# Feed forward input products as seven half-size products instead of eight, two of the weight sums made by accumulating DMAs

## Chip, cores, metric

One core of one Trainium2 chip. The metric is the device time of one execution in microseconds (us); less is better. The program runs two blocks of a network one after the other; the change is in the second.

## What is computed

The second block works on 512 tokens of width 1024, two layers deep. Each layer has two gated feed forward stages (`ffn`), so four in all, and they are most of its work:

```
def swiglu(x, w_in, w_out):
    a, b = jnp.split(x @ w_in, 2, axis=-1)
    return (jax.nn.silu(a) * b) @ w_out
...
    for i in range(DEPTH_2):
        h = h + FFN_RES * swiglu(rmsnorm(h, g_ff1[i]), w_ff1_in[i], w_ff1_out[i])
        h = h + hybrid_mixer(rmsnorm(h, g_mix[i]), ...)
        h = h + FFN_RES * swiglu(rmsnorm(h, g_ff2[i]), w_ff2_in[i], w_ff2_out[i])
```

`w_in` is 1024 x 5632 (the first 2816 columns give `a`, the others `b`), `w_out` is 2816 x 1024.

## The kernel before

Everything lies transposed: features on the 128 partitions, the 512 tokens along the free dimension. A feature width is cut into tiles of 128, so the input product of a stage has 22 **blocks** `j` (2816 / 128), and a block has two projections, `a` and `b`, each of 8 tiles of the inner width 1024. The 22 blocks are two halves of 11. After each half comes the output product (`fo`): 8 output tiles of 11 matmul triples.

Every factor is a pair of a rounded part and a rest (`whi`/`wlo` of a weight, `xh`/`xl` of an activation), and a product is three matmuls, hi\*hi, hi\*lo, lo\*hi (`mm3`, lines 156 to 159). So a block is 2 x 8 x 3 = 48 matmuls with 512 moving columns.

Weights come from one packed array in the order of use. `Stream` loads a group of eight 128 x 128 tiles by one DMA (`wraw`, 512 KB) and makes two units of four tiles of it: ScalarE (ACT) casts the rounded part `whi` (line 108), VectorE (DVE) subtracts for the rest `wlo` (line 109). `wraw`, `whi` and `wlo` have three buffers each. `get` keeps one unit ahead of the matmuls. At the end of a block DVE scales both projections by the norm's factor `R`, ACT takes Silu, DVE multiplies, and the product is split again for the output product (lines 338 to 342, 169, 170).

A scheduler orders the instructions of each engine when the program is built; `high_priority` lets an instruction go ahead of others. On the chip each engine then runs its own list in that order, and waits at an instruction whose operands or buffers aren't ready.

Of the kernel before, what the change touches and what calls it, by code (L numbers as in the profile page):

```python
# [19 lines left out]
HALF = NFF // 2  # L20
GRP = 8
UNIT = 4
# [7 lines left out]
TAPS1 = (1, 1, 2, 1)  # L30
TAPS2 = 12
CONV_AT = 5
NEG = -float(2 ** 100)
EPS = 1e-6

# [47 lines left out]
class Stream:  # L83


    def __init__(self, tc, pool, dram, order, whole=()):
        self.tc, self.nc, self.pool, self.dram, self.order, self.whole = tc, tc.nc, pool, dram, order, whole
        self.i = 0
        self.units = {}
        self.raw = {}  # L90

    def _load(self, u):
        nc = self.nc
        if u * UNIT >= len(self.order) or u in self.units:
# [29 lines left out]

    def prefetch(self):
        self._load(self.i // UNIT)

    def group(self, g, dst):

# [48 lines left out]
def block2(tc, kk, W, h, xp, x0, sq0, p_t, par, out_t):  # L178


    nc = tc.nc
    with ExitStack() as ctx:
        cp = ctx.enter_context(tc.tile_pool(name="b2c", bufs=1))
        mp = ctx.enter_context(tc.tile_pool(name="b2m", bufs=1))
        gp = ctx.enter_context(tc.tile_pool(name="b2g", bufs=1))
# [20 lines left out]

        qk2 = [[[cp.tile([66, S], F32R, name=f"{n}2{b}{i}") for n in "qk"] for i in range(2)] for b in range(2)]
        ones2 = tmp("ones2")[64:66]  # L210
        nc.vector.memset(ones2, 1.0)
        for b in range(2):
            for i in range(2):
                nc.vector.tensor_copy(qk2[b][i][0][64:66], ones2)
        maskr = cp.tile([P, P], F32R, name="maskr")
        mt = tmp("mt", (P, P))
        nc.gpsimd.memset(mt, 0.0)
# [7 lines left out]
        st = K()  # L225
# [32 lines left out]
        def norm(sq=None, n=1024):  # L258
            sq = st.sq if sq is None else sq
            ps = paux("ssps")  # L260
            nc.tensor.matmul(ps, lhsT=kk.ones[n], rhs=sq, start=True, stop=True)
            R = cp.tile([P, S], F32, tag="R", name="R", bufs=2)
            rstd(R, ps)
            return R

        def proj(name, l, col, ps=None, k_n=KD, x=None):
            ps = psum("pj") if ps is None else ps
            x = (xh, xl) if x is None else x
            for k in range(k_n):
# [53 lines left out]

            return R, scale_h

        def ffn(l, wi, wo, after, first=False):
            if first:
                R, scale_h = first_norm()
            else:
                R = norm()  # L330
            for half in range(2):
                gh, gl = [], []
                for jj in range(HALF):
                    j = half * HALF + jj
                    pa = proj(wi, l, j * P)
                    pb = proj(wi, l, FF + j * P)
                    a = tmp("fa")
                    nc.vector.tensor_tensor(a, pa, R, op=ALU.mult)  # L338
                    nc.scalar.activation(a, a, AF.Silu)
                    b = tmp("fb")  # L340
                    nc.vector.tensor_tensor(b, pb, R, op=ALU.mult)  # L341
                    nc.vector.tensor_tensor(b, a, b, op=ALU.mult)
                    g1 = gp.tile([P, S], F32R, tag=f"gh{jj}", name=f"gh{jj}")
                    g2 = gp.tile([P, S], F32R, tag=f"gl{jj}", name=f"gl{jj}")
                    split(nc, g1, g2, b)
                    gh.append(g1)
                    gl.append(g2)
                    if first and j == 3:
                        scale_h()
                for m in range(KD):  # L350
                    ps = psum("fo")
                    for jj in range(HALF):
                        w = W.get((wo, l, (half * HALF + jj) * P, m * P))
                        mm3(nc, ps, w, (gh[jj], gl[jj]), jj == 0, jj == HALF - 1)
                    nc.vector.scalar_tensor_tensor(h[m], ps, 0.5, h[m], op0=ALU.mult, op1=ALU.add)
                    if half == 1:
                        after(m)

        def gt(i, hl, name):
            return gp.tile([P, S], F32R, tag=f"g{hl}{i}", name=name)  # L360

        def mixer(l, after):
            R = norm()
            oh = [gt(i, "h", f"oh{i}") for i in range(4)]
            ol = [gt(i, "l", f"ol{i}") for i in range(4)]
            ca = []
# [267 lines left out]
                    after(m)  # L634

        for l in range(2):
            ffn(l, "w_ff1_in_2", "w_ff1_out_2", lambda m: prep(m, "g_mix", l), first=l == 0)
            mixer(l, lambda m: prep(m, "g_ff2", l))
            ffn(l, "w_ff2_in_2", "w_ff2_out_2", lambda m: prep(m, "g_ple", l))
# [897 lines left out]
def tile_main(tc, xt, ctxt, w1, w2, p1, p2, rcnt, pt, out_t, off1, off2):  # L1537
    nc = tc.nc
    with ExitStack() as ctx:
        cp = ctx.enter_context(tc.tile_pool(name="cp", bufs=1))  # L1540
        wp = ctx.enter_context(tc.tile_pool(name="wp", bufs=1))
        hp = ctx.enter_context(tc.tile_pool(name="hp", bufs=1))
        xp = ctx.enter_context(tc.tile_pool(name="xp", bufs=1))
        kk = K()
        kk.sqp = cp
        kk.paroff = off2
        make_consts(tc, kk, cp)
        par = cp.tile([P, p2.shape[1]], F32, name="par2")
        nc.sync.dma_start(par, p2)
        W1 = Stream(tc, wp, w1, order1(), whole=("w_mod",))  # L1550
        W2 = Stream(tc, wp, w2, order2())
# [12 lines left out]
        block2(tc, kk, W2, h, xp, x0, sq0, pt, par, out_t)  # L1564

# [35 lines left out]
```

## Time and profile before

| | |
|---|---|
| median of 3 runs | 2983.14 us (2980.09 to 2984.42) |
| the profiled execution | 2981.43 us, of which its span 2979.7 us |
| granted TensorE clock, mean | 0.995 of 2.4 GHz |
| TensorE (PE) busy | 2934.9 us, 98% |
| DVE busy | 1910.1 us, 64% |
| ACT busy | 1298.3 us, 44% |

The span is from the first to the last instruction of the profiled execution. Busy is the union of an engine's instruction times; matmuls overlap in the pipeline of PE, so a single one lasts longer than the distance from one to the next.

### The profile page before, as it was taken

How to read it: one execution, taken by the hardware profiler on the slowest of the kernel's cores; microseconds unless marked ns; L12 is line 12 of the kernel's file. 1: busy time of each engine (PE TensorE's matmuls, PEld its weight loads, DVE VectorE, ACT ScalarE, POOL GpSimd, SP SyncE). 2: the span in 40 equal slices, each digit the busy share in tenths (PEclk: the TensorE clock that was granted, in tenths of full speed). 3: DMA queues.
4: the chain of work that ended last, by engine and by line, in shares of the span. 5: the costliest groups of instructions: out<-in, count | busy, mean ns of one | idle time of the engine just before them, and what ended most of it. 6: DMA issues, size and time to landing. Idle time of an engine off the chain costs nothing.

```text
span 2979.7 us, 37937 instructions
## 1 busy us (share of the span) xinstructions
PE 2934.9 (98%) x13992; PEld 2392.2 (80%) x13992; DVE 1910.1 (64%) x3753; ACT 1298.3 (44%) x2387; POOL 48.1 (2%) x105
## 2 busy tenths in 40 slices
PE   8999999999999999999999999999999999999998
PEld 5888887778888887688888888888888688888886
DVE  6788888787544469886543447444469886543446
ACT  6567766435323335544432335323335544432333
POOL 1000000000000000000000000000000000000000
PEclk9999999999999999999999999999999999999999
DMA  5211123233233332123333333333232123233332
GB/s 216 57 42 47 45 58 106 92 92 92 92 99 98 94 99 85 50 85 99 94 98 99 96 95 102 97 99 98 94 99 84 50 87 99 92 99 98 94 99 85
DMA packets 112986, 268.77 MB, mean 90 GB/s; under 512 B 43552, under 2 KB 47136, under 8 KB 112800
## 3 DMA queue, kind: packets, MB, share of 16 engines
q1 hardware_dynamic: 111776, 266.28, 28.8%
q8 instruction: 110, 1.80, 0.2%
q14 instruction: 76, 0.62, 0.1%
q0 software_dynamic: 1024, 0.07, 0.0%
HBM read 262.17 MB, written 4.06 MB: 89 GB/s over the span
## 4 chain that ended last, share of the span: by engine, by line
PE 93%; DVE 3%; ACT 2%; issue 1%; DMA 0%; SPq 0%; DVEq 0%; ACTq 0%
PE pj L158 17%; PE pj L157 17%; PE pj L159 17%; PE fo L158 5%; PE fo L157 5%; PE fo L159 5%; PE px L157 3%; PE px L158 3%; PE px L159 2%; PE o L486 1%; PE wo L158 1%; PE mX L1285 1%; PE wo L159 1%; PE mP L1290 1%; PE wo L157 1%; PE chn L1337 1%
## 5 line engine op out<-in xcount | busy, mean ns | idle before, releaser
L108 ACT CAST whi<-wraw 128x512 fp32r<-128x512 f32 x914 | 567.1, 621 | 1163.9 <-PE pj L158 699.3
L109 DVE TENSOR_TENSOR wlo<-wraw,whi 128x512 fp32r<-128x512 f32 x914 | 627.3, 687 | 446.1 <-ACT whi L108 423.6
L158 PE MATMUL pj<-xl,whi 128*128 128x512 f32 x1712 | 672.6, 393 | 0.0
L157 PE MATMUL pj<-xh,whi 128*128 128x512 f32 x1712 | 670.5, 392 | 0.9 <-DVE h L1526 0.9
L159 PE MATMUL pj<-xh,wlo 128*128 128x512 f32 x1712 | 669.3, 391 | 0.0
L159 PEld LDWEIGHTS pj<-xh,wlo 128*128 128x128 f32 x1712 | 321.9, 188 | 67.9 <-issue 2.3
L158 PEld LDWEIGHTS pj<-xl,whi 128*128 128x128 f32 x1712 | 322.2, 188 | 66.9 <-issue 2.7
L157 PEld LDWEIGHTS pj<-xh,whi 128*128 128x128 f32 x1712 | 322.2, 188 | 66.4 <-ACT whi L108 1.3
L157 PE MATMUL fo<-gh,whi 128*128 128x512 f32 x704 | 273.9, 389 | 0.0
L158 PE MATMUL fo<-gl,whi 128*128 128x512 f32 x704 | 273.9, 389 | 0.0
L159 PE MATMUL fo<-gh,wlo 128*128 128x512 f32 x704 | 273.9, 389 | 0.0
L420 DVE SCALAR_TENSOR_TENSOR cy<-ca,par,cy 128x489 f32<-128x489 f32 (+17 forms) x240 | 169.6, 729 | 1.5
L157 PE MATMUL px<-xh,whi 128*128 128x512 f32 x392 | 160.3, 409 | 0.8 <-ACT xh L1000 0.7
L158 PE MATMUL px<-xl,whi 128*128 128x512 f32 x392 | 160.6, 410 | 0.0
L159 PE MATMUL px<-xh,wlo 128*128 128x512 f32 x392 | 159.1, 406 | 0.0
L157 PEld LDWEIGHTS fo<-gh,whi 128*128 128x128 f32 x704 | 132.1, 188 | 27.5
L159 PEld LDWEIGHTS fo<-gh,wlo 128*128 128x128 f32 x704 | 132.1, 188 | 27.5
L158 PEld LDWEIGHTS fo<-gl,whi 128*128 128x128 f32 x704 | 132.1, 188 | 27.4
L341 DVE TENSOR_TENSOR fb<-pj,R 128x512 f32<-128x512 f32 x88 | 60.8, 691 | 129.9 <-PE pj L159 129.9
L338 DVE TENSOR_TENSOR fa<-pj,R 128x512 f32<-128x512 f32 x88 | 60.8, 691 | 125.4 <-PE pj L159 123.5
L157 PE MATMUL pj<-nh,whi 128*128 128x512 f32 x352 | 137.3, 390 | 0.0
L158 PE MATMUL pj<-nl,whi 128*128 128x512 f32 x352 | 137.0, 389 | 0.0
(427 smaller groups left out, 4473.4 us busy)
## 6 DMA issues: line engine op xcount, KB each, us to landing
wraw<-in_w_dram SPq DMA_DIRECT2D x465, 512.0 KB
mw<-in_w_dram SPq DMA_DIRECT2D x16, 512.0 KB
raw<-in_xt_dram SPq DMA_DIRECT2D x8, 256.0 KB
h<-in_xt_dram SPq DMA_DIRECT2D x8, 256.0 KB
out_dram<-fin SPq DMA_DIRECT2D x8, 256.0 KB
db<-B SPq DMA_DIRECT2D x64, 6.0 KB
Pm<-dq SPq DMA_DIRECT2D x64, 12.0 KB
Qm<-dq SPq DMA_DIRECT2D x64, 12.0 KB
```

The lines of the kernel that those rows point to most:

```text
L108: nc.scalar.copy(hi, src)
L109: nc.vector.tensor_tensor(lo, src, hi.bitcast(F32), op=ALU.subtract)
L157: nc.tensor.matmul(ps, lhsT=wh, rhs=xh, start=start, stop=False)
L158: nc.tensor.matmul(ps, lhsT=wh, rhs=xl, start=False, stop=False)
L159: nc.tensor.matmul(ps, lhsT=wl, rhs=xh, start=False, stop=stop)
L338: nc.vector.tensor_tensor(a, pa, R, op=ALU.mult)
L341: nc.vector.tensor_tensor(b, pb, R, op=ALU.mult)
L420: nc.vector.scalar_tensor_tensor(yy[:, s:], ca[cb][:, :S - s], pcol("conv_w", l, cb, j), yy[:, s:], op0=ALU.mult, op1=ALU.add)
L486: nc.tensor.matmul(po_[r, kb * P:], lhsT=vt[kb][:, hp * P + 64 * i:hp * P + 64 * i + 64], rhs=pts[i], start=kb == 0, stop=kb == 3)
L1285: nc.tensor.matmul(pX[:, o], lhsT=st.B[:, m0 + m], rhs=alt(st.Q, m0 + m), start=True, stop=True)
L1290: nc.tensor.matmul(pP[:, o], lhsT=Xt[:, m], rhs=alt(st.P, m0 + m), start=True, stop=True)
L1337: nc.tensor.matmul(pa, lhsT=st.kN[:, c], rhs=y2, start=True, stop=True)
```

## The change

Blocks 0 to 4 of each stage stay as they are (`plain`). From block 5 on, a block is one 2 x 2 product of matrices of halves: the weights' two projections (256 rows out) by the two halves of the inner width, times the activations' two halves of the inner width by the two halves of the tokens. It is computed by seven products of halves where eight were computed. A product is 4 inner tiles x 3 matmuls with 256 moving columns, so a block has 84 matmuls of 256.

- `operand(kk)`, four times per stage during the plain blocks, builds the activations' side: two normed tiles, four sums and differences of halves, and the splits of all (7 tiles each time).
- `squares` loads a block's weights: four plain loads on the SP queue (one of 512 KB, three of 256 KB), and two accumulating DMAs of 256 KB on the GpSimd (POOL) queue that add a quarter to the quarter already loaded (`s1`, `s3`). `weight` makes the other two sums on DVE (`s2`, `s4`) and splits each of the seven operands (128 x 512) on ACT and DVE. Their pairs go round eight buffers, which the plain blocks' activations held.
- `sevens` computes the seven products in the order a11, a12, s1, s2, s3, a22, s4, two to a PSUM bank (`sv`), and adds them up: ACT copies the first and the third out (`u`), DVE makes seven additions of 128 x 256, then ACT Silu, DVE multiply and split as before. Weights are prepared five products ahead in the text (`LEAD`).
- The second operands of the mixer (`qk2`) are set up anew in each mixer, since their buffers serve as operand buffers in between.

The number of columns streamed by PE falls from 48 x 512 to 84 x 256 per block, for 17 blocks in each of 4 stages: 68 blocks. Core of the diff:

```diff
+PLAIN = 5
+LEAD = 5
...
+    def squares(self, i, spare):
+        nc, g, H = self.nc, i // GRP, UNIT * P
+        x = self.pool.tile([P, GRP * P], F32, tag="wraw", name="wraw", bufs=3)
+        nc.sync.dma_start(x, self.dram[g])
+        s1 = self.pool.tile([P, H], F32, tag="whi", name="ws1", bufs=3)
+        nc.sync.dma_start(s1, self.dram[g + 1][:, :H])
+        s3 = spare()
+        nc.sync.dma_start(s3, self.dram[g][:, :H])
+        nc.gpsimd.dma_start(s1, self.dram[g + 1][:, H:], accum_op=ALU.add)
+        nc.gpsimd.dma_start(s3, self.dram[g + 1][:, :H], accum_op=ALU.add)
+        a22 = self.pool.tile([P, H], F32, tag="wlo", name="wa22", bufs=3)
+        nc.sync.dma_start(a22, self.dram[g + 1][:, H:])
+        return dict(a11=x[:, :H], a12=x[:, H:], s1=s1, s3=s3, a22=a22)
...
+            def operand(kk):
+                ab = []
+                for k in (kk, 4 + kk):
+                    t = tmp("xn")
+                    nc.vector.scalar_tensor_tensor(t, h[k], pcol(gname, l, k), R, op0=ALU.mult, op1=ALU.mult)
+                    ab.append(t)
...
+            def weight(j, name):
+                r = raws[j]
+                with tc.high_priority():
+                    if name == "s2":
+                        nc.vector.tensor_tensor(r["a11"], r["a11"], r["s1"], op=ALU.add)
+                        src = r["a11"]
+                    elif name == "s4":
+                        nc.vector.tensor_tensor(r["a12"], r["a12"], r["a11"], op=ALU.add)
+                        src = r["a12"]
+                    else:
+                        src = r[name]
+                    hi, lo = pair(turn[0] % 8, alt)
+                    turn[0] += 1
+                    split(nc, hi, lo, src)
+                return hi, lo
+
+            def sevens(js, half, at, then):
+                steps = [(n, name) for n in range(len(js)) for name in ("a11", "a12", "s1", "s2", "s3", "a22", "s4")]
...
+                for i in range(LEAD):
+                    prepare(i)
+                for i, (n, name) in enumerate(steps):
+                    prepare(i + LEAD)
...
+                    if name in ("a11", "s1", "s3", "s4"):
+                        bank[:] = [psum("sv") if turns[0] % 2 else paux("sv"), 0]
+                        turns[0] += 1
+                    o = bank[0][:, H * bank[1]:H * bank[1] + H]
...
+                    for kk in range(4):
+                        w = slice(kk * P, kk * P + P)
+                        mm3(nc, o, (wh[:, w], wl[:, w]), ops[rhs[name], kk], kk == 0, kk == 3)
+                    if name == "a11":
...
+                        nc.scalar.copy(u1, o)
+                    elif name == "a12":
+                        nc.vector.tensor_tensor(h1, o, u1, op=ALU.add)
+                    elif name == "s1":
+                        nc.scalar.copy(u2, o)
+                    elif name == "s2":
+                        nc.vector.tensor_tensor(u1, o, u1, op=ALU.add)
+                        nc.vector.tensor_tensor(h2, u1, u2, op=ALU.add)
+                    elif name == "s3":
+                        nc.vector.tensor_tensor(v1, o, u1, op=ALU.add)
+                        nc.vector.tensor_tensor(v2, v1, u2, op=ALU.add)
+                    elif name == "a22":
+                        nc.vector.tensor_tensor(v1, o, v1, op=ALU.add)
+                    else:
+                        nc.vector.tensor_tensor(h2, o, h2, op=ALU.add)
+                        nc.scalar.activation(st.h, st.h, AF.Silu)
+                        nc.vector.scalar_tensor_tensor(st.h, st.v, -1.0, st.h, op0=ALU.mult, op1=ALU.mult)
+                        hidden(js[n] - half * HALF, st.h)
...
             for half in range(2):
...
+                for j in range(lo_, min(PLAIN, lo_ + HALF)):
+                    if j == PLAIN - 1:
+                        load(js[0], first_at)
+                    plain(j - lo_, j)
+                    if j < 4:
+                        operand(j)
                     if first and j == 3:
                         scale_h()
+                sevens(js, half, first_at, out_at)
```

**How the lists of the engines change.** First PE, inside the second half of the first stage. Before, a block was 48 matmuls in a row with one wait per unit. Now PE's list mixes the products: the end of a11 of one block (`xh6` is its weight pair's rounded part), eight matmuls of s1 (`xh0`), then the first of a12 (`xh7`), into the bank `sv_10186` that a11 filled.

```order
L185 MATMUL sv_10186<-xs_8181,xl6_10086 128x256
L183 MATMUL sv_10235<-sl1_7871,xh0_10121 128x256
L184 MATMUL sv_10235<-sh2_7880,xh0_10121 128x256
L185 MATMUL sv_10235<-sl1_7871,xl0_10122 128x256
L183 MATMUL sv_10235<-sh5_7984,xh0_10121 128x256
L184 MATMUL sv_10235<-sl5_7985,xh0_10121 128x256
L185 MATMUL sv_10235<-sh5_7984,xl0_10122 128x256
L183 MATMUL sv_10235<-xs_8089,xh0_10121 128x256
L184 MATMUL sv_10235<-xs_8090,xh0_10121 128x256
L183 MATMUL sv_10186<-sl0_7867,xh7_10103 128x256 [waits Activation_49]
```

The last row waits for ACT, though its weights were cast before those of s1: it waits for the copy out of its bank.

ACT, before, around a block of the feed forward: casts of the stream's units, one Silu, one split.

```order
L339 ACTIVATE fa_13805<-fa_13805 128x512 [waits DVE_49]
L108 CAST whi_13816<-wraw_13787 128x512 [waits PE_49,Activation_49]
L108 CAST whi_13834<-wraw_13832 128x512 [waits DMAHW0_49,PE_49,Activation_49]
L169 CAST gh5_13811<-fb_13808 128x512 [waits DVE_49]
L108 CAST whi_13851<-wraw_13832 128x512 [waits PE_49,Activation_49]
```

And now, at the place of the PE rows above. `xh4`, `xh6`, `xh7`, `xh0` are casts of the weights of s4 of this block and a12, s1, s2 of the next; `u_10199` are the two copies out of PSUM.

```order
L195 CAST xh4_10204<-wraw_9929 128x512 [waits PE_49]
L195 CAST xh6_10249<-wraw_10075 128x512 [waits PE_49,Activation_49]
L501 COPY u_10199<-sv_10186 128x256 [waits PE_49]
L195 CAST gh3_10178<-hid_10054 128x512 [waits DVE_49]
L195 CAST xh7_10267<-ws1_10077 128x512 [waits DMASW5_49,PE_49,Activation_49]
L195 CAST xh0_10287<-wraw_10075 128x512 [waits PE_49,Activation_49]
L505 COPY u_10199<-sv_10235 128x256 [waits PE_49]
```

Each copy stands behind a cast into the pair that a product just ending on PE still reads (pairs go round by eight, so the cast of a12 of the next block takes the pair of a11 of this one).

DVE at the same place: between the addition that reads s2 (line 507) and the one that reads s3 (line 510) stand the sum behind it and two splits for the next block.

```order
L507 TENSOR_TENSOR u_10199<-sv_10235,u_10199 128x256 [waits DVE_49,PE_49,Activation_49]
L508 TENSOR_TENSOR hid_10200<-u_10199 128x256 [waits DVE_49]
L196 TENSOR_TENSOR xl1_10305<-s3_10079,xh1_10304 128x512 [waits DMASW0_49,Activation_49]
L196 TENSOR_TENSOR xl2_10329<-wa22_10083,xh2_10328 128x512 [waits DMAHW6_49,PE_49,Activation_49]
L510 TENSOR_TENSOR v_10201<-sv_10271,u_10199 128x256
```

Last, DVE at the passage from block 4 (plain) to block 5 in the very first stage: `xl6_8528` and `xl7_8546` are weights of block 7, `fa_8291` and `fb_8294` read the results of plain block 4, `hid_8350` is the first addition of block 5, `xl1_8418` the rest of s1 of block 6.

```order
L196 TENSOR_TENSOR xl7_8546<-wraw_8371,xh7_8545 128x512 [waits PE_49,Activation_49]
L351 TENSOR_TENSOR h3_5812<-h3_5812,Rh_8202 128x512
L454 TENSOR_TENSOR wraw_8371<-wraw_8371 128x512 [waits DVE_49]
L351 TENSOR_TENSOR h4_5814<-h4_5814,Rh_8202 128x512
L351 TENSOR_TENSOR h5_5816<-h5_5816,Rh_8202 128x512
L351 TENSOR_TENSOR h6_5818<-h6_5818,Rh_8202 128x512
L351 TENSOR_TENSOR h7_5820<-h7_5820,Rh_8202 128x512
L431 TENSOR_TENSOR fa_8291<-pj_8227,R_7769 128x512
L434 TENSOR_TENSOR fb_8294<-pj_8262,R_7769 128x512
L435 TENSOR_TENSOR fb_8294<-fa_8291,fb_8294 128x512 [waits DVE_49,Activation_49]
L196 TENSOR_TENSOR gl4_8298<-fb_8294,gh4_8297 128x512 [waits Activation_49]
L503 TENSOR_TENSOR hid_8350<-sv_8336,u_8349 128x256 [waits PE_49]
```

The scaling of `h`, which before lay inside a long row of plain blocks, now stands between weights of a block far ahead and the first results that PE's banks wait to be read.

## Rows read from the trace of the kernel before

**Rows 1.** The page's first part: engine, busy us, share of the span, instructions.
```profile
PE 2934.9 (98%) x13992; PEld 2392.2 (80%) x13992; DVE 1910.1 (64%) x3753; ACT 1298.3 (44%) x2387; POOL 48.1 (2%) x105
```

**Rows 2.** The page's 40 equal slices: busy tenths of PE, granted clock.
```profile
PE   8999999999999999999999999999999999999998
...
PEclk9999999999999999999999999999999999999999
```

**Rows 3.** The chain that ended last, as shares of the span.
```profile
PE 93%; DVE 3%; ACT 2%; issue 1%; DMA 0%; SPq 0%; DVEq 0%; ACTq 0%
```

**Rows 4.** Timeline within one feed forward block: start us, us long, engine, line, operation.
```profile
1502.36 0.39 PE L158 MATMUL pj<-xl,whi 128*128 128x512 f32 x1
...
1502.84 0.62 ACT L108 CAST whi<-wraw 128x512 fp32r<-128x512 f32 x1 [1.19 <-PE pj L158]
...
1503.49 0.69 DVE L109 TENSOR_TENSOR wlo<-wraw,whi 128x512 fp32r<-128x512 f32 x1 [1.91 <-ACT whi L108]
...
1506.34 0.68 DVE L109 TENSOR_TENSOR wlo<-wraw,whi 128x512 fp32r<-128x512 f32 x1
...
1506.94 0.68 DVE L342 TENSOR_TENSOR fb<-fa,fb 128x512 f32<-128x512 f32 x1
...
1507.66 0.62 ACT L169 CAST gh<-fb 128x512 fp32r<-128x512 f32 x1 [1.49 <-DVE fb L342]
...
1508.28 0.62 ACT L108 CAST whi<-wraw 128x512 fp32r<-128x512 f32 x1
...
1508.31 0.69 DVE L170 TENSOR_TENSOR gl<-fb,gh 128x512 fp32r<-128x512 f32 x1 [0.69 <-ACT gh L169]
...
1510.74 0.39 PE L159 MATMUL pj<-xh,wlo 128*128 128x512 f32 x1
...
1510.97 0.39 PE L157 MATMUL pj<-xh,whi 128*128 128x512 f32 x1
...
1511.17 0.69 DVE L338 TENSOR_TENSOR fa<-pj,R 128x512 f32<-128x512 f32 x1 [1.54 <-PE pj L159]
```

**Rows 5.** Timeline of PE in the first block, matmuls of 256 columns.
```profile
60.74 0.28 PE L157 MATMUL pc<-cx,whi 128*128 128x256 f32 x1
60.85 0.28 PE L158 MATMUL pc<-cx,whi 128*128 128x256 f32 x1
60.97 0.28 PE L159 MATMUL pc<-cx,wlo 128*128 128x256 f32 x1
61.09 0.40 PE L157 MATMUL px<-xh,whi 128*128 128x512 f32 x1
```

**Rows 6.** Groups by form, operations of 256 columns: count, busy us, mean ns.
```profile
L831 ACT COPY u<-pc 128x256 f32<-128x256 f32 x16 | 5.8, 371 | 6.3 <-PE pc L159 3.7 <-PE chn L1324 2.5
L1229 DVE TENSOR_TENSOR B<-B,KK 128x256 f32<-128x256 f32 x8 | 3.3, 410 | 0.0
```

**Rows 7.** Timeline of DVE, two operations of which the second reads the first.
```profile
1098.01 0.69 DVE L255 SCALAR_TENSOR_TENSOR rs<-ssps,rs 128x512 f32<-128x512 f32 x1
1098.74 0.69 DVE L256 SCALAR_TENSOR_TENSOR R<-rs,R 128x512 f32<-128x512 f32 x1
```

**Rows 8.** Timeline, a matmul whose weights DVE makes at the last moment.
```profile
502.50 0.34 DVE L1330 SCALAR_TENSOR_TENSOR rhs<-chn,negeG,vN 128x128 f32<-128x128 f32 x1
...
502.90 0.30 PEld L1333 LDWEIGHTS chn<-rhs,Pm 128*128 128x128 f32 x2 [0.36 <-DVE rhs L1330]
502.90 0.49 PE L1333 MATMUL chn<-rhs,Pm 128*128 128x128 f32 x2
503.11 0.30 PEld L1350 LDWEIGHTS po<-y,QK 128*128 128x128 f32 x2
```

**Rows 9.** Busy time in one feed forward stretch: PE, PEld, DVE, ACT, POOL, clock, DMA share, GB/s.
```profile
725.00:840.00 115.00, 114.75 (x521) 95.27 (x522) 62.22 (x112) 42.68 (x68) 0.50 (x2) 1.00 0.29 92
```

**Rows 10.** DMA issues on POOL's queue: size, median us to landing.
```profile
k<-cs POOLq DMA_DIRECT2D x32, 2.0 KB, 1.6
```

More of the change, by code (lines that the diff above doesn't have):

```diff
@@ L324, in first_norm, with pair, extra, ffn @@
             return R, scale_h
-        def ffn(l, wi, wo, after, first=False):
+        def pair(i, alt):
+            if alt:
+                return mtile(2 * i, f"sh{i}"), mtile(2 * i + 1, f"sl{i}")
+            return tuple(xp.tile([P, S], F32R, tag=f"x{n}{i}", name=f"x{n}{i}") for n in "hl")
+        def extra(i):
+            tags = [f"{n}2{b}{j}" for b in range(2) for j in range(2) for n in "qk"] + ["pe3", "pe3", "cs", "x28"]
+            return cp.tile([P, S], F32R, tag=tags[i], name="xs", bufs=2 if tags[i] == "pe3" else 1)
+        def ffn(l, gname, wi, wo, after, first=False, alt=False):
             if first:
@@ L330, in ffn @@
                 R = norm()
-            for half in range(2):
[L332 to L347, printed above, removed]
+            H = S // 2
@@ new lines, in ffn, with slot @@
+            ops = {}
+            base = W.i
+            used = []
+            def slot():
+                n = len(used)
+                used.append(n)
+                if n < 16:
+                    if n % 2 == 0:
+                        used_pair[:] = pair(n // 2, not alt)
+                    return used_pair[n % 2]
+                return extra(n - 16)
+            used_pair = []
+            def operand(kk):
[4 more added lines that the diff above has]
+                    ab.append(t)
+                x, y = ab
+                b11, b12, b21, b22 = x[:, :H], x[:, H:], y[:, :H], y[:, H:]
+                t = slot()
+                split(nc, t[:, :H], t[:, H:], b11)
+                ops["b11", kk] = t[:, :H], t[:, H:]
+                hi, lo = slot(), slot()
+                split(nc, hi, lo, y)
+                ops["b21", kk] = hi[:, :H], lo[:, :H]
+                ops["b22", kk] = hi[:, H:], lo[:, H:]
+                u = tmp("t12")
+                nc.vector.tensor_tensor(u[:, :H], b11, b12, op=ALU.subtract)
+                nc.vector.scalar_tensor_tensor(u[:, H:], u[:, :H], -1.0, b22, op0=ALU.mult, op1=ALU.subtract)
+                v = tmp("t34")
+                nc.vector.tensor_tensor(v[:, :H], b22, b12, op=ALU.subtract)
+                nc.vector.scalar_tensor_tensor(v[:, H:], u[:, H:], -1.0, b21, op0=ALU.mult, op1=ALU.subtract)
+                for t, names in ((u, ("t1", "t2")), (v, ("t3", "t4"))):
+                    hi, lo = slot(), slot()
+                    split(nc, hi, lo, t)
+                    ops[names[0], kk] = hi[:, :H], lo[:, :H]
+                    ops[names[1], kk] = hi[:, H:], lo[:, H:]
@@ new lines, in hidden, with plain @@
+            def hidden(jj, g):
+                g1 = gp.tile([P, S], F32R, tag=f"gh{jj}", name=f"gh{jj}")
+                g2 = gp.tile([P, S], F32R, tag=f"gl{jj}", name=f"gl{jj}")
+                split(nc, g1, g2, g)
+                gs[jj] = g1, g2
+            def plain(jj, j):
+                pa = proj(wi, l, j * P)
+                pb = proj(wi, l, FF + j * P)
+                a = tmp("fa")
+                nc.vector.tensor_tensor(a, pa, R, op=ALU.mult)
+                nc.scalar.activation(a, a, AF.Silu)
+                b = tmp("fb")
+                nc.vector.tensor_tensor(b, pb, R, op=ALU.mult)
+                nc.vector.tensor_tensor(b, a, b, op=ALU.mult)
+                hidden(jj, b)
@@ new lines, in ffn, with load @@
+            raws = {}
+            def load(j, at):
+                if j not in raws:
+                    raws[j] = W.squares(at, lambda: cp.tile([P, S], F32, tag="R", name="s3", bufs=2))
+            turn = [0]
+            def weight(j, name):
[13 more added lines that the diff above has]
+                return hi, lo
@@ new lines, in sevens, with prepare @@
+            def sevens(js, half, at, then):
+                steps = [(n, name) for n in range(len(js)) for name in ("a11", "a12", "s1", "s2", "s3", "a22", "s4")]
+                rhs = dict(a11="b11", a12="b21", s1="t1", s2="t2", s3="t3", s4="b22", a22="t4")
+                ready = {}
+                live = {}
+                bank = []
+                turns = [0]
+                def prepare(i):
+                    if i < len(steps):
+                        n, name = steps[i]
+                        if name == "a11":
+                            for q in (n, n + 1):
+                                if q < len(js):
+                                    load(js[q], at + 16 * q)
+                        ready[i] = weight(js[n], name)
+                for i in range(LEAD):
+                    prepare(i)
+                for i, (n, name) in enumerate(steps):
+                    prepare(i + LEAD)
+                    if i == len(steps) - 7:
+                        W.ahead(then)
+                    st = live.setdefault(n, K())
+                    if name in ("a11", "s1", "s3", "s4"):
+                        bank[:] = [psum("sv") if turns[0] % 2 else paux("sv"), 0]
+                        turns[0] += 1
+                    o = bank[0][:, H * bank[1]:H * bank[1] + H]
+                    bank[1] += 1
+                    wh, wl = ready.pop(i)
+                    for kk in range(4):
+                        w = slice(kk * P, kk * P + P)
+                        mm3(nc, o, (wh[:, w], wl[:, w]), ops[rhs[name], kk], kk == 0, kk == 3)
+                    if name == "a11":
+                        st.u, st.h, st.v = tmp("u"), tmp("hid"), tmp("v")
+                        u1, u2, h1, h2, v1, v2 = (t[:, e * H:e * H + H] for t in (st.u, st.h, st.v) for e in range(2))
+                        nc.scalar.copy(u1, o)
[16 more added lines that the diff above has]
+                        hidden(js[n] - half * HALF, st.h)
+                        live.pop(n)
+                W.i = then
@@ new lines, in ffn @@
+            for half in range(2):
+                gs = {}
+                lo_ = half * HALF
+                js = list(range(max(lo_, PLAIN), lo_ + HALF))
+                out_at = base + (half + 1) * HALF * 16 + half * KD * HALF
+                first_at = out_at - 16 * len(js)
+                for j in range(lo_, min(PLAIN, lo_ + HALF)):
[4 more added lines that the diff above has]
+                        operand(j)
@@ L348, in ffn @@
                     if first and j == 3:
                         scale_h()
+                sevens(js, half, first_at, out_at)
                 for m in range(KD):
+                    if half == 0 and m == KD - 1:
+                        load(HALF, out_at + KD * HALF)
                     ps = psum("fo")
@@ L363, in mixer @@
             R = norm()
+            qk2 = second_operands()
             oh = [gt(i, "h", f"oh{i}") for i in range(4)]
```

31 lines of the change are left out of this document (19 added, 12 removed).

## The prediction

> **What bounds the kernel now.** The page's first part comes first: PE is busy 98% of the span, DVE 64%, ACT 44% [rows 1]. The slices show PE at 9 tenths everywhere at a full clock [rows 2], and the chain of work that ended last lies on PE for 93% [rows 3]. So nothing but PE's own work counts, and the question is how densely PE issues matmuls. The timeline within a block answers it: from the L158 at 1502.36 to the L157 at 1510.97 are 38 matmuls of 512 columns, 0.2267 us each [rows 4]. A block of 48 takes 10.88 us, and no engine makes PE wait in it: ACT's cast at 1502.84 was released by a matmul, not the other way round. In that stretch DVE is busy 54% and ACT 37% of the time [rows 9]: both have room, which the change is about to use.
>
> **The change, part by part.**
>
> *Matmuls.* 84 of 256 columns replace 48 of 512. Three in a row in the first block take 61.09 - 60.74 = 0.35 us, 0.1167 each [rows 5]; half of 0.2267 would be 0.1134. I take 0.1167, a measured distance of that very form: 84 x 0.1167 = 9.80 us per block, 1.08 less than 10.88, times 68 blocks **-73.4 us**. With 0.1134 it is -92, with 0.120 -54. At 0.1295 nothing would be won. [...]
>
> *DVE and ACT.* Queued DVE operations of 512 columns start 0.60 apart (1506.34, 1506.94) though each lasts 0.68 [rows 4]; one of 256 lasts 0.41 [rows 6], so 0.33 apart; one that reads the operation just before starts 0.73 after it [rows 7], 0.04 after its end. Per new block DVE has 7 splits, 2 sums, a multiply and a last split (11 x 0.60) and 7 additions (7 x 0.33 and 0.12 for the one that waits): about 9.0 us. ACT has 9 casts and splits or Silu at 0.62 and 2 copies at 0.37 [rows 4, 6]: 6.3 us. Neither is above PE's 9.80, but both must now answer PE several times in each block.
>
> *New waits.* The lists show three kinds per block: a12 waits for ACT's copy of a11, s2 for the copy of s1, a22 for DVE's reading of s3. None is for data that the product uses; two products share a bank. I price each as the path from PE's last release to the waiting matmul, less the matmuls that stand between in PE's list. The pieces: a matmul of 256 lasts 0.28 [rows 5]; ACT starts 0.09 after the end of the matmul that frees its buffer (1502.36 + 0.39 to 1502.84), DVE 0.04 after (1510.74 + 0.39 to 1511.17) [rows 4]; PE resumes 0.06 after DVE (502.50 + 0.34 to 502.90) [rows 8].
> - a12: the cast of the next a12 can start when a11's eleventh matmul ends, and the copy stands behind it: 0.28 + 0.09 + 0.62 + 0.37 + 0.06 = 1.42 us. From that matmul's start PE has 2 + 8 matmuls to do: 1.17. Wait 0.25.
> - s2: from a12's eleventh: two casts, then the copy, 0.37 + 1.24 + 0.37 + 0.06 = 2.04, against 2 + 4 + 9 matmuls, 1.75. Wait 0.29.
> - a22: from s2's last: 0.32 to DVE, line 507 and its dependent 508 (0.45 + 0.33), two splits (1.20), line 510 (0.41), 0.06: 2.77, against 1 + 3 + 12 + 7 matmuls, 2.68. Wait 0.09.
>
> Sum 0.63. The order repeats every three blocks; in the other two ACT's Silu and further casts stand ahead of the copies. At a12 the path grows by two and by three of them, to 2.67 and 3.29, and PE has 19 and 24 matmuls to cover it (2.22 and 2.80). At s2 it is 1.61 from a12's start against 12 (1.40), and 2.04 against 14 (1.63). At a22 2.87 against 24 and 2.77 against 23. They wait 0.45 + 0.21 + 0.07 and 0.49 + 0.41 + 0.09. Mean 0.78 per block: **+53 us** over 68. DVE keeps up in this timetable, with about 1.5 us idle per block.
>
> *Restart.* Where a wait holds the weight load too, the first matmul comes one load later: the pair of loads in [rows 8] lasts 0.30, one 0.19, so 0.11 per wait. In an unheld stream the load runs ahead. The waiting matmuls here have old weights, so I take 0; the other bound is 3 x 0.11 x 68 = +22.
>
> *Passage from the plain blocks.* In the first stage ACT's first copy (u of block 5) stands behind casts for blocks 6 and 7. By the same pieces PE stops 1.2 us at a12 of block 5. Then s2 needs the second copy, which follows the Silu of plain block 4, which follows `fa`, which follows line 351 five times and a sum, which follow `xl7`; and that split ends about when a12 does. Six operations of 0.60, `fa`, Silu and copy with 0.7, 0.65 and 0.4 make some 5.1 us of waiting; with 1.2 in front and behind, 7.5. The other stages have no line 351 there: 0.75 us for the last operand splits and 1.95 at a12, behind four casts and a Silu, 2.7 each. Together **+15.6**; no row of before shows this, so between 8 (half) and 24 (half more).
>
> *Ends of the halves.* The last block has no next one to fill its waits: some 0.3, eight times, **+2.4**.
>
> *Operands.* 4.9 us of DVE per plain block for four blocks, on top of 4.8 (8 operations at 0.60): 9.7 of 10.88. Hidden, since the stream's splits stay a unit ahead in DVE's list; if that cover goes, at most 4 us per stage.
>
> *Transfers.* A plain block loads 0.5 + 0.5 MB, a new one 1.3 MB by plain loads and 0.5 MB by accumulating ones. At the stretch's price, 0.29 of the DMA engines for 92 GB/s [rows 9], 1.83 MB in 10.6 us take 0.54 of them. The s3 buffers (two) are freed some 20 us before they are needed, and I see POOL's small DMAs land in 1.6 us [rows 10]. No row shows an accumulating one; at the price of a load it costs nothing, at four times it 0.29 x (1.31 + 4 x 0.52)/(92 x 10.6/1000) = 1.0, and the engines are full: there it begins to decide. The Trainium skill (DMA: Bandwidth & Descriptors, section Anatomy of one DMA) fits 2.0 us + bytes / 436 GB/s for a DMA from GpSimd; by this estimate a load and an accumulation take 5.2 us, well within the buffers' time. No run here has shown it.
>
> *Sum:* -73.4 + 53 + 15.6 + 2.4 = **-2.4 us**, 2979.0 against the profiled execution's 2981.43, which is 1.7 below the median shown; say **2980**.
>
> **Rivals.** *A, the forecast:* the waits give back nearly all. Its own range takes 0.1134 and 0.120 per matmul (faster matmuls wait longer: about half of the difference stays, -9 and +9) and the passages: 2964 to 2996.
> *B, the waits are covered:* if ACT's and DVE's releases come earlier than my pieces (0.25 us at each wait would do for the first kind), only passages and ends remain: -73.4 + 18 = -55, **2926**; half covered 2953. For it: the scheduler put 8 to 14 matmuls in just these gaps. Against it: every piece is measured.
> *C, slower by the restart:* each of the nine waits in three blocks costs a weight load as well, 0.11 us. It decides above 0.04 us per wait; in full it gives -2.4 + 22 = +20, **3001**. For it [rows 8]; against it, that there the late operand is the weight.
> *D, the accumulating DMAs are the bound:* at 4.6 times a load's price they fill 11.7 us per block, 1.1 over the 10.6 of A, +75: **3055**. Against it the 20 us between.
> *E, the products aren't cheaper:* 0.1295 or more per matmul of 256. [Rows 5] speak against it; it is within D's chance.
>
> **How the numbers follow.** A 0.45 (of that 0.15 faster, 0.20 same, 0.10 slower), B 0.27, C 0.18, D with E 0.10. Faster by over 0.2% (6 us, about what a measurement tells from no change): 0.15 + 0.27 = 0.42. Same 0.20. Slower 0.10 + 0.18 + 0.10 = 0.38. The range must leave out no more than 0.2: D is left out above (0.10) and the fully covered end of B below (about 0.08): 2930 to 3015.
>
> **What would show it.** Per block: the distance of `sv` matmuls where nothing waits (0.1134 to 0.120); the time of three blocks in the second half (31.7 us by A, 29.4 by B, 32.7 by C); idle PE before L183 released by ACT `u` and DVE `v`; the restart in the load after such a wait. In the first stage a gap of about 5 us on PE some 3 us after it starts a12 of block 5, released by ACT `u`. DMA share near 0.54 in the second halves, and no DVE wait on L451 released by a DMA. The prediction is wrong if PE's matmuls of 256 columns last longer beside so much DVE and DMA work, if DVE falls behind by more than its 1.5 us, or if the banks aren't what a12 waits for.

## The result, and the profile after

The changed kernel takes **3036.78 us** (median of 4 runs, 3033.17 to 3038.93), the kernel before 2981.98 in the same session: ratio 1.0182, 95% interval 1.0164 to 1.0200. The forecast was 2980 with a range of 2930 to 3015, so it missed, and on the slow side. The profiled execution took 3033.17 us, its span is 3031.5 against 2979.7: 51.8 us more.

The page of the changed kernel, busy times, slices of PE and clock, and one row on DMA issues:

```profile
PE 2923.4 (96%) x16440; PEld 2488.6 (82%) x16440; DVE 2269.3 (75%) x4598; ACT 1468.2 (48%) x2791; POOL 166.0 (5%) x241
...
PE   8999999999899999999999999999999999999998
...
PEclk9999999999999999999999999999999999999999
...
ws<-in_w_dram POOLq DMA_DIRECT2D x68, 256.0 KB, 5.3
```

PE is busy 11.5 us less than in [rows 1], and yet the span grew. The slices, which answer to [rows 2], hide why: what PE lost is in gaps too short for a slice of 76 us. So the stretches of sevens have to be measured one by one, each from its first `sv` matmul to the first `fo` matmul behind it. First the four first halves (6 blocks each), then the four second halves (11 blocks), by windows; columns as in [rows 9]:

```profile
780.35:858.96 78.61, 67.13 (x505) 65.11 (x504) 61.44 (x116) 33.94 (x64) 10.39 (x12) 0.91 0.55 145
...
sum 292.36, PE 258.84 PEld 253.35 DVE 230.86 ACT 136.35 POOL 41.49; mean PE 64.71 PEld 63.34 DVE 57.72 ACT 34.09 POOL 10.37
```
```profile
1633.78:1759.42 125.64, 117.66 (x926) 114.19 (x924) 100.09 (x193) 61.01 (x116) 15.59 (x18) 0.97 0.58 146
...
sum 500.00, PE 471.23 PEld 457.13 DVE 401.13 ACT 244.52 POOL 62.31; mean PE 117.81 PEld 114.28 DVE 100.28 ACT 61.13 POOL 15.58
```

292.36 + 500.00 = 792.4 us for 68 blocks; at 10.88 each they took 739.8 before. That is +52.5, the whole difference: it lies in these eight stretches and nowhere else. The mean clock in them is 0.91 to 0.97, not 1.00.

Inside a second half, away from its start, PE's timeline shows a wait as this pattern:

```profile
1672.98 0.28 PE L184 MATMUL sv<-sh,xh 128*128 128x256 f32 x1
...
1676.69 0.19 PEld L184 LDWEIGHTS sv<-xs,xh 128*128 128x128 f32 x1
1676.81 0.28 PE L184 MATMUL sv<-xs,xh 128*128 128x256 f32 x1
1676.99 0.19 PEld L183 LDWEIGHTS sv<-sl,xh 128*128 128x128 f32 x1
1676.99 0.38 PE L183 MATMUL sv<-sl,xh 128*128 128x256 f32 x1
1677.21 0.28 PE L184 MATMUL sv<-sh,xh 128*128 128x256 f32 x1
1677.33 0.28 PE L185 MATMUL sv<-sl,xl 128*128 128x256 f32 x1
...
1700.51 0.28 PE L184 MATMUL sv<-sh,xh 128*128 128x256 f32 x1
```

From 1672.98 to 1676.81 are 32 matmuls without a wait: 0.1197 us each. The matmul at 1676.99 comes 0.18 after the one ahead (0.06 of waiting), the next 0.22 after that (0.10 more). The weight load of the waiting matmul is held with it: it starts at 1676.99 too, where the load before it starts 0.12 ahead of its matmul. Three blocks, from 1668.79 to 1700.51 at the same place of the pattern, take **31.72 us**. In them are nine such pairs: the waits sum to 0.65 us, the longer distances behind them to 0.91. The window over the three:

```profile
1668.79:1700.51 31.72, 31.72 (x254) 30.69 (x253) 27.97 (x55) 17.48 (x34) 5.22 (x6) 1.00 0.72 174
```

At the start of each half it looks different. The timeline of a second half, all engines, some matmuls of PE left out (PE began the sevens at 1633.78):

```profile
1628.70 0.86 POOL L148 DMA_DIRECT2D ws<-in_w_dram  x1 [53.12 <-PE fo L185]
...
1631.03 0.33 SPq L145 DMA_DIRECT2D ws<-in_w_dram  x1
...
1632.90 0.62 ACT L195 CAST xh<-ws 128x512 fp32r<-128x512 f32 x1 [3.42 <-DMA ws<-in_w_dram]
...
1635.93 0.36 ACT L501 COPY u<-sv 128x256 f32<-128x256 f32 x1
...
1636.73 0.86 POOL L148 DMA_DIRECT2D ws<-in_w_dram  x1 [7.17 <-DVE xl L196]
...
1639.21 0.28 PE L184 MATMUL sv<-xs,xh 128*128 128x256 f32 x1
...
1645.06 0.69 DVE L451 TENSOR_TENSOR wraw<-wraw,ws 128x512 f32<-128x512 f32 x1 [7.63 <-DMA ws<-in_w_dram]
1645.12 0.62 ACT L195 CAST xh<-ws 128x512 fp32r<-128x512 f32 x1 [8.82 <-DMA ws<-in_w_dram]
...
1646.39 0.37 ACT L505 COPY u<-sv 128x256 f32<-128x256 f32 x1
...
1646.81 0.58 PE L183 MATMUL sv<-sl,xh 128*128 128x256 f32 x1 [7.32 <-ACT u L505]
```

ACT does nothing from 1636.3 to 1645.1. At the head of its list stands the cast of s1 of the *second* block (12), whose accumulating DMA POOL issued at 1636.73 and which lands at 1645.0. Behind it stands the copy (L505) that frees the bank of s1 of the *first* block (11), and PE waits 7.32 us for that. ACT's list shows it; the first and the last row are block 11:

```
L501 COPY u_16375<-sv_16362 128x256 [waits PE_49]
L195 CAST xh3_16443<-ws1_16329 128x512 [waits DMASW2_49,PE_49]
L195 CAST xh4_16463<-wraw_16327 128x512 [waits DVE_49,PE_49,Activation_49]
L505 COPY u_16375<-sv_16411 128x256 [waits PE_49]
```

In a first half it is DVE's list, here in the second stage: the sum for s2 of block 6 (L451) waits for the same kind of DMA, and the last operand (L414) that PE needs for block 5 stands behind it.

```profile
1511.54 0.69 DVE L451 TENSOR_TENSOR wraw<-wraw,ws 128x512 f32<-128x512 f32 x1 [7.30 <-DMA ws<-in_w_dram]
1512.14 0.42 DVE L414 SCALAR_TENSOR_TENSOR t<-t,xn 128x256 f32<-128x256 f32 x1
...
1512.60 0.62 ACT L195 CAST xs<-t 128x512 fp32r<-128x512 f32 x1 [9.15 <-DVE t L414]
...
1513.27 0.58 PE L183 MATMUL sv<-xs,xh 128*128 128x256 f32 x1 [7.42 <-ACT xs L195]
```

There are nine gaps, 3.60 to 7.42 us, one in each half and two in the first: 53.7 us in all. Eight wait for a late sum; the second of the first half, 4.19 us, is the one behind the scaling of `h` that the prediction priced. Behind the gaps PE runs slow. Windows over the gap and the time after it (the clock is the third column from the right):

```profile
1639.00:1646.80 7.80, 0.49 (x5) 0.29 (x3) 1.71 (x4) 1.51 (x3) 0.86 (x1) 0.83 0.87 176
1646.81:1651.00 4.19, 4.19 (x19) 4.19 (x20) 2.33 (x6) 1.20 (x2) 0.46 (x1) 0.50 0.22 66
```

After the gap the granted clock is 0.50, the lower level of 1.2 GHz, and matmuls come every 0.21 us. Over the eight stretches some 170 matmuls ran so, 17 us more than at 0.12. Gaps and slow matmuls make 71 us.

### The profile page after: what moved, and what is told of

Its sections match the earlier page's. It is cut to its first block, busy times and chain, and to the rows that moved or that the text cites. A ratio compares the mean times of both kernels' runs of the same rounds, so it can differ in the third digit from the quotient of the medians.

```text
span 3031.5 us, 45013 instructions
## 1 busy us (share of the span) xinstructions
PE 2923.4 (96%) x16440; PEld 2488.6 (82%) x16440; DVE 2269.3 (75%) x4598; ACT 1468.2 (48%) x2791; POOL 166.0 (5%) x241
## 5 line engine op out<-in xcount | busy, mean ns | idle before, releaser
L112 ACT CAST whi<-wraw 128x512 fp32r<-128x512 f32 x642 | 396.8, 619 | 722.4 <-PE pj L184 275.2
L113 DVE TENSOR_TENSOR wlo<-wraw,whi 128x512 fp32r<-128x512 f32 x642 | 439.9, 686 | 262.5 <-ACT whi L112 246.8
L184 PE MATMUL pj<-xl,whi 128*128 128x512 f32 x896 | 355.4, 397 | 0.0
L183 PE MATMUL pj<-xh,whi 128*128 128x512 f32 x896 | 353.2, 394 | 0.9 <-DVE h L1716 0.9
L185 PE MATMUL pj<-xh,wlo 128*128 128x512 f32 x896 | 352.1, 393 | 0.0
L185 PEld LDWEIGHTS pj<-xh,wlo 128*128 128x128 f32 x896 | 169.0, 189 | 35.9 <-issue 2.3
L184 PEld LDWEIGHTS pj<-xl,whi 128*128 128x128 f32 x896 | 169.0, 189 | 35.5 <-issue 2.7
L183 PEld LDWEIGHTS pj<-xh,whi 128*128 128x128 f32 x896 | 169.2, 189 | 34.4 <-ACT whi L112 1.3
L184 PE MATMUL sv<-xs,xh 128*128 128x256 f32 x663 | 190.4, 288 | 6.1 <-DVE xs L196 6.1
L183 PE MATMUL sv<-xs,xh 128*128 128x256 f32 x561 | 161.4, 288 | 13.1 <-ACT xs L195 13.1
L185 PE MATMUL sv<-xs,xl 128*128 128x256 f32 x561 | 155.8, 288 | 0.0
```

## The experiments

All times are medians of 4 runs, the ratios those to the kernel before. The last two columns are sums of the four first and the four second halves, measured as above; in 6 to 9 without the 0.8 us of eight small matmuls that the moved scaling of `h` puts ahead of one `fo`.

| kernel | us | ratio, 95% interval | first halves | second halves |
|---|---|---|---|---|
| the change | 3036.78 | 1.0182 (1.0164 to 1.0200) | 292.4 | 500.0 |
| 1 no accumulating DMAs | 2965.95 | 0.9946 (0.9931 to 0.9961) | 262.4 | 463.0 |
| 2 a bank per product | 2969.27 | 0.9956 (0.9939 to 0.9973) | 282.4 | 444.5 |
| 3 sums on POOL | 3060.70 | 1.0263 (1.0248 to 1.0279) | 302.9 | 517.5 |
| 4 sums on DVE | 3033.81 | 1.0170 (1.0155 to 1.0186) | 308.1 | 483.8 |
| 5 both 1 and 2 | 2939.41 | 0.9852 (0.9835 to 0.9868) | 250.0 | 443.5 |
| 6 2, and two moves in order | 2955.78 | 0.9909 (0.9894 to 0.9923) | 270.2 | 443.5 |
| 7 the two moves alone | 3013.98 | 1.0103 (1.0088 to 1.0118) | 270.2 | 499.1 |
| 8 2, DVE sums in blocks 6 and 7 | 2950.55 | 0.9897 (0.9881 to 0.9914) | 263.7 | 443.5 |
| 9 2, DVE sums in block 6 | 2942.15 | 0.9861 (0.9845 to 0.9878) | 257.5 | 444.1 |

**1. Without the accumulating DMAs**

```diff
-        nc.gpsimd.dma_start(s1, self.dram[g + 1][:, H:], accum_op=ALU.add)
-        nc.gpsimd.dma_start(s3, self.dram[g + 1][:, :H], accum_op=ALU.add)
```

> This kernel leaves out the two accumulating DMAs of each block: s1 and s3 are used as their plain loads alone (so the products are of other data, all other work is as in the changed kernel). Theory 1, late accumulations: the gaps of 3.6 to 7.4 us that PE has once or twice in each half, some 3 to 10 us after it begins the sevens, come from ACT's cast and DVE's sum that stand at the head of their lists and wait for s1 to land. They add up to 53.7 us, and after each PE runs about 20 matmuls at 0.21 instead of 0.12 us, some 2 us, nine times. Without the accumulations 45 to 70 us go away: 2965 to 2990 us. Theory 2, late buffers: the plain load of s1 waits for a whi buffer that the output product or the plain blocks still hold, and lands too late by itself: gaps of over 3 us stay in most halves, 3010 to 3030 us. Theory 3, the steady blocks are the cost: three blocks in the second half take 31.72 us in any case, 3030 us or more.

71 us less: theory 1 holds. The sums of the windows over the second halves, and what is left of gaps in the first stage:

```profile
sum 463.01, PE 462.85 PEld 449.62 DVE 389.23 ACT 240.26 POOL 0.00; mean PE 115.71 PEld 112.40 DVE 97.31 ACT 60.07 POOL 0.00
```
```profile
794.57 0.58 PE L181 MATMUL sv<-sl,xh 128*128 128x256 f32 x1 [4.65 <-ACT u L503]
```

The second halves have no gap any more: 10.52 us per block with all the bank waits in them. The gap of 4.65 at s2 of block 5 in the first stage is the one that the prediction had at 5.1. With the data in time, the kernel is what was forecast, or a little better.

**2. A bank for each product**

```diff
-                    if name in ("a11", "s1", "s3", "s4"):
+                    if True:
                         bank[:] = [psum("sv") if turns[0] % 2 else paux("sv"), 0]
```

> Each of the seven products has a PSUM bank of its own (half of it unused), nothing else is changed in the text. If a12 and s2 wait for copies out of the bank that they share, the wait (0.05 to 0.15 us) and the double distance of the matmul behind it (0.22 instead of 0.12) go away: three blocks 31.72 -> about 30.2 us (252 matmuls at 0.1197), so 0.5 us per block, 34 us over 68 blocks: about 3003 us, with the gaps at the start of the halves as they are. If instead DVE or ACT is what PE follows, three blocks stay above 31.3 us and the time above 3025. If more banks in flight let a product start later than now, it gets slower.

68 us less, twice what was expected. The windows over one second half and all four:

```profile
2027.48:2138.35 110.87, 110.87 (x925) 110.87 (x924) 98.61 (x193) 58.74 (x116) 15.60 (x18) 1.00 0.65 165
...
sum 444.49, PE 444.02 PEld 443.59 DVE 396.66 ACT 239.31 POOL 62.36; mean PE 111.00 PEld 110.90 DVE 99.16 ACT 59.83 POOL 15.59
```

110.87 us are 924 matmuls at 0.1200: neither waits nor restarts are left. The 0.5 per block was the expected part; the other is that the gaps of the second halves are gone too, though s1 is accumulated as before. The copy still stands behind the late cast, but nobody waits for its bank. So a gap there needs both, a late sum and a shared bank. In the first halves the gaps stay (four of them released by DVE `xs`, 25.7 us), where the bank plays no part.

**3 and 4. The sums on an engine.** For 4, `gpsimd` is `vector`:

```diff
-        nc.gpsimd.dma_start(s1, ..., accum_op=ALU.add)
-        nc.gpsimd.dma_start(s3, ..., accum_op=ALU.add)
...
+        with self.tc.high_priority():
+            nc.gpsimd.tensor_tensor(s3, s3, s1, op=ALU.add)
+            nc.gpsimd.tensor_tensor(s1, s1, a22, op=ALU.add)
```

> s1 and s3 are summed by POOL (two additions of 128x512 per block) from plain loads of all four quarters, in place of the accumulating DMAs; the output is the same. Late accumulations: the gaps of 3.6 to 7.4 us shrink to below 2 us if POOL's addition takes less than about 3 us, DMA share in the steady blocks falls from 0.72 to about 0.5, and the time is 2965 to 2995 us. Late buffers: gaps stay, 3010 to 3030. If POOL's additions slow DVE's operations down (now 0.68 us, 9.3 of 10.6 us per block), DVE becomes the bound: over 3030 us and DVE operations above 0.75 us.

Slower still, by its third case. The groups in one second half (count, busy, mean ns), the window of it, and DVE and POOL in a piece of the timeline:

```profile
L152 POOL TENSOR_TENSOR ws<-ws,wa 128x512 f32<-128x512 f32 x10 | 15.9, 1587 | 0.8
```
```profile
L197 DVE TENSOR_TENSOR sl<-wraw,sh 128x512 fp32r<-128x512 f32 x41 | 39.6, 983 | 0.6
...
L197 DVE TENSOR_TENSOR sl<-s,sh 128x512 fp32r<-128x512 f32 x10 | 6.9, 687 | 0.0
```
```profile
2081.00:2209.00 128.00, 115.91 (x919) 111.44 (x918) 114.29 (x191) 59.55 (x114) 28.96 (x20) 1.00 0.33 108
```
```profile
2118.28 1.30 POOL L151 TENSOR_TENSOR s<-s,ws 128x512 f32<-128x512 f32 x1 [7.73 <-issue]
2118.35 0.41 DVE L516 TENSOR_TENSOR hid<-sv,hid 128x256 f32<-128x256 f32 x1
2118.68 1.45 DVE L197 TENSOR_TENSOR sl<-wraw,sh 128x512 fp32r<-128x512 f32 x1
2119.66 1.62 POOL L152 TENSOR_TENSOR ws<-ws,wa 128x512 f32<-128x512 f32 x1
2120.05 1.78 DVE L197 TENSOR_TENSOR sl<-wraw,sh 128x512 fp32r<-128x512 f32 x1
```

Two splits that take 1.29 us in a queue took 3.15, each beside an addition on POOL (1.30 and 1.62 us) and each ending 0.55 us after it; the same line with another operand kept its 0.687. DVE is busy 89% of the stretch, and PE waits in nearly every block.

> The same two sums on DVE instead of POOL (two more operations of 128x512 per block, 0.60 us each in a queue). Late accumulations: the gaps at the start of the halves go away, but DVE's 9.3 us per block become 10.5 of 10.57: three blocks take 31.7 to 33 us, the time is 2970 to 3010 us. Late buffers: gaps of over 3 us stay and DVE is full besides: 3030 to 3060 us.

Neither case in full: the time lies in the range of the second, 3030 to 3060, but not by its gaps. The second halves cost 10.99 per block, 33.0 for three, the upper end of what DVE's load was to give (it is busy 109.30 of 121.00 us between 921 and 1042). But the first halves were worse than with the accumulations: no gap above 2.6 us outside the first stage (5.5 there), and many of 0.5 to 2.6.

**5. Both edits of 1 and 2**

> Both edits of the first two experiments: a bank for each product, and the accumulating DMAs left out (s1 and s3 are their plain loads alone, so the products are of other data). With the accumulations gone the six gaps of 5.1 to 7.4 us that a bank for each product left in the first halves (31.5 us, and about 7 us of matmuls at half the clock) should go, except about 5 us in the first stage, where the scaling of h stands ahead; the blocks stay at 10.09 us. 2969 - 31.5 - 7 + 5 = about 2936 us. If the gaps of the first halves come from something else than the late sum, they stay: 2965 or more.

As expected (of the gaps it names there are five, not six): three first halves at 60.71 to 60.89 us, and in the first stage one gap of 5.0 released by DVE `fa`. The window of one first half:

```profile
1481.42:1542.13 60.71, 60.71 (x505) 60.52 (x504) 56.23 (x110) 34.47 (x65) 0.00 (x0) 1.00 0.42 135
```

With a bank each the second halves take 444.5 us with the accumulations (experiment 2) and 443.5 without: their traffic alone costs next to nothing. In the second halves edit 1 alone takes 37.0 us away, edit 2 alone 55.5, both together 56.5: 36 us are the gaps that either of them removes.

**6 and 7. The order**

```diff
-                with tc.high_priority():
+                with nullcontext() if j == PLAIN + 1 else tc.high_priority():
...
-                    if first and j == 3:
-                        scale_h()
                 sevens(js, half, first_at, out_at)
+                if first and half == 0:
+                    scale_h()
```

> A bank for each product, the accumulating DMAs as in the changed kernel (the output is the reference's), and two moves in the order: the weights of the second block of sevens in a first half (block 6) are prepared without high priority, so that in DVE's and ACT's lists they come after the last operands and after the results of plain block 4; and h is scaled after the sevens of the first half and not in the middle of the passage. If the gaps of the first halves are only the wait for the late s1 standing ahead of work that has its data, all of them go, though the transfers are as late as before: 2969 - 31.5 - 7 = about 2931 us, 2925 to 2942. If s1 itself is late for its product, a gap of 2 us or more stays in each first half: 2945 or more.

> The two moves in the order alone, with two products to a bank as in the changed kernel. The gaps of the second halves (6.7, 7.5, 7.0, 3.8 us and half the clock after each, some 32 us) stay, since there the copy still stands behind the cast that waits for s1; in the first halves the gaps of 6.3 and 4.4, 7.6, 6.1, 5.9 us go or are cut to below 2 us. 3037 - 30 - 8 = about 3000 us; if in the first halves too a copy out of a shared bank comes to stand behind a late cast, they stay and it is 3020 or more.

Experiment 7: the second halves as they were (499.1), the first halves 22 us shorter where 38 were expected, with a gap of 3.6 to 4.3 us left in three of the four, released by DVE `v`. Experiment 6 gives 13 of its 38 us. The timeline of 6 at the second passage shows why:

```profile
1477.33 0.85 POOL L149 DMA_DIRECT2D ws<-in_w_dram  x1 [10.94 <-DVE xl L197]
...
1485.73 0.62 ACT L196 CAST xh<-ws 128x512 fp32r<-128x512 f32 x1 [7.10 <-DMA ws<-in_w_dram]
1486.26 0.62 ACT L433 ACTIVATE fa<-fa 128x512 f32<-128x512 f32 x1
1486.79 0.35 ACT L502 COPY u<-sv 128x256 f32<-128x256 f32 x1
...
1488.85 0.55 PE L186 MATMUL sv<-sh,xl 128*128 128x256 f32 x1 [2.52 <-DVE xl L197]
```

DVE's list was mended, ACT's not: the cast of the late s1 now stands ahead of the Silu of plain block 4 and of the copies. The wait moved one engine on and shrank from 7 to 1.7 to 4.5 us.

**8 and 9. The late sums on DVE, only in the passage.** `squares` gets a flag; where it is set, DVE makes s1 and s3 as in experiment 4. With a bank per product, and the scaling of `h` moved:

> A bank for each product, h scaled after the sevens of the first half, and in each first half the sums s1 and s3 of the second and third block of sevens (6 and 7) made by DVE from plain loads instead of by accumulating DMAs; all other blocks accumulate as in the changed kernel, and the output is the reference's. If what is left in the first halves of the experiment with a bank for each product (gaps of 5.1 to 7.4 us) is the wait for the accumulation of block 6, made slow by those of 7 and 8 that are sent together with it, the gaps go: 2969 - 31.5 - 7 = 2931 us, plus DVE's 4 additions of 0.6 us beside PE: 2930 to 2940 us. If plain loads are late too in that burst, gaps of 2 us or more stay: 2945 to 2960.

> The same with DVE making the sums of block 6 alone; block 7 accumulates. If only the very first accumulation in the passage is late, this is as fast as with two blocks, 2930 to 2940 us; if that of block 7 is late in its turn, the gaps move one block on and shrink, since there is one more block of matmuls (10.09 us) before them: 2940 to 2955 us.

Block 6 alone is better than 6 and 7: in experiment 8 PE waits 2.3 to 2.7 us in each first half for a DVE addition (L508) that stands behind the additional sums. So its time lies in its second range, but not by late plain loads. Experiment 9 falls into its second range, 2940 to 2955: what is left are waits for a copy, 0.9 us at the passage and 0.6 to 2.3 a block later, the longest behind a cast that waits 5.08 us for an accumulated s3. It leaves nothing out, and beats the kernel before by 1.4% and the change by 95 us. One first and one second half of it:

```profile
1473.73:1540.12 66.39, 62.82 (x505) 62.19 (x504) 57.17 (x112) 33.94 (x65) 8.61 (x10) 0.97 0.64 164
1599.99:1710.86 110.87, 110.87 (x925) 110.87 (x924) 98.48 (x193) 58.35 (x116) 15.61 (x18) 1.00 0.66 165
```

## Why the prediction was wrong, by its own steps

The sum of the forecast beside what the changed kernel's stretches show, in us:

| term | forecast | measured | from |
|---|---|---|---|
| matmuls | -73.4 | -56.1 | 84 x 0.1197 = 10.05, less 10.88, x 68 |
| waits in a block | +53 | +14.7 | 0.65 in three blocks |
| restart | 0 | +20.6 | 0.91 in three blocks |
| passages plain to sevens | +15.6 | +38.6 | 292.4 - 24 x 10.573 |
| second halves | +2.4 | +34.8 | 500.0 - 44 x 10.573 |
| sum | -2.4 | +52.6 | stretches: +52.5 |

- **Blocks: sum right, parts wrong.** Three blocks take 31.72, forecast A said 31.7 (B 29.4, C 32.7). But that is luck of three errors. The matmul is 0.1197, not 0.1167: three distances between rows that are rounded to 0.01 [rows 5] leave it open from 0.113 to 0.120, and the upper end of my range was the right one. Half of 0.2267 was never a bound to lean on: 0.2267 - 0.1197 = 0.107 is 256 columns at 2.4 GHz, and the remaining 0.013 is paid per matmul at both widths. By the formula that the Trainium skill (TensorE: Matmul & The Clock Gate, section Back-to-back issue gap) gives for an isolated matmul, this width takes 109 ns; no run here shows it.
- **Waits.** All nine exist and fall on the banks, as the lists said: with a bank each they vanish. They are 0.07 us on average, not 0.26; my pieces overrate them.
- **Restart.** Taken as 0 with 0.11 as the bound; it is 0.10 behind each wait. Rival C had the mechanism, a wait that holds the weight load too, and old weights did not spare it.
- **Engines.** DVE 9.3 us per block (estimate 9.0), ACT 5.8 (6.3): fine, and DVE's room of 1.3 us carried the blocks.
- **Passage of the first stage.** The gap at s2 of block 5 was predicted at 5.1 us (its pieces add up to 5.35): 4.65 where nothing else is late (experiment 1). The wait at a12 of block 5 ahead of it is there too, 0.9 of idle time (predicted 1.2). Without accumulations all four passages cost 262.4 - 24 x 10.52 = 9.9 us, within the range of 8 to 24.
- **Transfers: the step that failed.** I priced the accumulating DMAs at nothing, by their share of the DMA engines and by the s3 buffers' 20 us. The share was 0.72 in the three blocks rather than 0.54, and even that costs nothing there (experiments 2 and 5). The error is where it was not looked at: s1 has no 20 us at a passage. It takes `whi` buffers which the plain blocks or the output product hold to their end, so load and accumulation of the next blocks start together when these end, and the second one's s1 lands 8.5 to 11.3 us after the sevens begin. PE needs it only at about 13 us. But its cast and its sum go with high priority and stand in ACT's and DVE's lists ahead of copies and operands that PE needs at 5 us. All my release paths assumed that whatever stands ahead in a list has its data. Without the accumulations the kernel is 71 us faster (experiment 1). The sign that the prediction named, a DVE wait on L451 released by a DMA, came: 7.63 us at 1645.06, 7.30 at 1511.54.
- **Second halves.** The passage from the output product to the sevens was not counted at all; it has the same late s1, and costs nearly as much.
- **Rival D** came nearest in time (3055) for a wrong reason: the accumulations are not a bound on throughput, they are late at eight places. A run has now shown their time: 5.3 us in the median, 8.3 in the passage shown. By the Trainium skill (DMA: Bandwidth & Descriptors, section Anatomy of one DMA; 2.0 us + bytes / 436 GB/s) the estimate was 5.2 us for a load and an accumulation together, so 2.6 each; the accumulation alone took twice its part.

What stays open: how much of the 8 us in a passage is the transfer itself and how much the other loads sent with it. The windows from issue to landing of two accumulations of 256 KB in the half shown, of the first block and of the second, give a part of the answer (the DMA share is the second column from the right):

```profile
1628.70:1632.88 4.18, 4.18 (x21) 3.44 (x20) 1.29 (x2) 0.78 (x2) 0.86 (x1) 1.00 0.62 143
1636.73:1645.04 8.31, 2.76 (x24) 2.56 (x22) 0.70 (x2) 0.00 (x0) 2.59 (x3) 0.95 0.85 201
```

So about half of it was the transfer with fewer others beside it. No run sent an accumulation alone.

## What to carry to other kernels

An operation that waits for a transfer costs what stands *behind* it in its engine's list, not what needs its result: look, at each change of stage, at what a prepared-ahead operation is ahead of. A buffer shared between stages dates the first transfers of the next stage, so count lead time there and not in the steady run. And two results in one PSUM bank make an eviction a condition for the next product: a bank each was worth 68 us here, half of it in waits of a tenth of a microsecond.

## What the runs showed of the hardware that was not expected

- After a gap of 7.3 us PE came back at a granted clock of 0.50 and kept it for about 4 us: 1.9 us on top of the gap. After the one of 3.6 us it was 2.5 us: in proportion a short gap cost more.
- Each short wait of PE is followed by a distance of 0.22 instead of 0.12 us, though the weights were in their buffer: the load that runs ahead of its matmul was held with it.
- Accumulating DMAs of 256 KB landed 3.6 to 9.3 us after POOL issued them.
- DVE and POOL hold each other up. The Trainium skill (SBUF — State Buffer, section Who interferes with whom) says that a DVE operation with both inputs in SBUF contends with a GpSimd one that reads SBUF, and that the ports which the two share are an exclusive lock. Experiment 3 agrees: two splits took 3.15 us instead of 1.29, each ending 0.55 us after the addition beside it, and the addition that began during a split took 1.62 us where the other took 1.30. An addition on DVE with one input in PSUM (L516) kept its 0.41 us beside POOL. POOL's DMA issues (0.86 us) did nothing of the kind: DVE's splits kept 0.685 us beside them.
